# Two-layer hybrid block on one core: another written order in the mixer, and raw compressed keys copied out of their bank

## The chip, the cores and the metric

The kernel runs on one core of one Trainium2 chip. The metric is the device time of one launch in microseconds (us), lower is better. Times of the kernel before come from three timed runs and from one execution recorded by the hardware profiler.

## What is computed

The reference is a two-layer block over 256 tokens of width 1024. Cut to what matters here:

```python
for l in range(2):
    x = x + 0.5 * swiglu_ffn(x, ...)                 # 1024 -> 2816 -> 1024
    h = rms_norm(x, mix_norm[l])
    o_a = fox_mixer(...)      # 4 heads, softmax with a forget bias        (jobs F0, F1)
    o_b = gmlp_mixer(...)     # gated unit with a 128x128 token mix
    o_c = nsa_mixer(...)      # selected + window softmax (jobs N0..N3) and attention to 15 compressed keys
    o_d = pool_mixer(...)     # moving averages, then a product
    x = x + concat(o_a, o_b, o_c, o_d) @ w_out[l]
    x = x + 0.5 * swiglu_ffn(x, ...)

# compressed keys and values, inside nsa_mixer
flat  = blocks_of_32_tokens + pos_emb                # 15 x 2048
k_cmp = rope(rms_norm(gelu(flat_k @ k_w1) @ k_w2))   # 15 x 64
v_cmp = gelu(flat_v @ v_w1) @ v_w2
p_cmp = softmax(q @ k_cmp.T, masked);  o_cmp = p_cmp @ v_cmp
```

With 256 tokens and blocks of 64 every block is among the top ones, so the selection needs no gather: job pairs N0/N1 and N2/N3 are the selected and the window branch of two heads each.

## The kernel before

Each layer is FFN, mixer, FFN. A 32-bit weight tile is loaded by SP's queue, copied into a rounded half `h` on ScalarE (L122), and the rest `lo` is formed on VectorE (L123). TensorE then takes three products per pair of tiles (`mm3`, L143 to L145) or two passes (`mm2x2`, L151 and L153). `raws` holds 4 loaded tiles, `spl` 4 split ones, and `banks` the 8 accumulator banks, which `bank_a` and `bank_h` hand out; a tile waits for a bank until every reader of an earlier tile in it is through.

In the mixer small blocks of attention lie between blocks of long products that need nothing from them. A softmax job goes through six steps: `scores` (eight TensorE instructions into two banks L774, then maxima on VectorE L782 and exponentials with sums on ScalarE L784), `scale` (L790 to L795, VectorE), `trans` (six transpose passes L802 into two banks, copied to memory by ScalarE L804), `values` (L814), `done` (the accumulator is split into halves for the output product, L134 on ScalarE and L135 on VectorE). The compressed branch runs over `cmp_hidden` (four loads and product groups, L462), `cmp_gelu`, `cmp_out` (values into `vbd`, L505; raw keys, their squares L511, and after a `yield` their scaling and rotation L514 to L522), `cmp_keys` (L527), `cmp_scores` (L731 to L751), `cmp_weights` (L758).

The long blocks are generators: `go(w00, 4)` takes the next four steps of `out_part(0, 0)`, twelve products. The first step of `out_part` (and of `b_proj`, `z_proj`) only loads and splits the weights. `w00` and `w10` use the gate and pool outputs (`oT` 2, 3, then 6, 7), `w01` and `w11` use the fox outputs (`oT` 0, 1) and then the compressed/selected/window outputs (`oT` 4, 5). `wacc` and `wacc1` are the two pairs of banks for the output product.

From `here` to `pin(here)` each instruction on TensorE, VectorE and ScalarE is chained behind the one written before it on the same engine, so the written order is the order of these three queues. Instructions written after that stretch (the splits of the next FFN) are not chained and may be put between. SP and GpSimd are not chained.

Of the kernel before, what the change touches and what calls it, by code (L numbers as in the profile page):

```python
# [70 lines left out]
def tile_macaron(ctx, tc, xT, g0, const0, consts, params, w13, w2, wA, wB, wD, wC, wE, wcmp, wo, out):  # L71
# [15 lines left out]
    def bank_a():  # L87
        a = banks.tile([128, 512], F32, name="a", tag="bank")
        return a

    def bank_h():
        h = banks.tile([128, 512], F32, name="h", tag="bank")
        return h
# [5 lines left out]
    def halves(s):  # L99
        return s.rearrange("p (a n) -> p a n", a=2)  # L100
# [87 lines left out]
    def inv_rms(ss, n, width, p=128):  # L188

        ms = wk.tile([128, 16], F32)  # L190
        nc.gpsimd.tensor_scalar(ms[:p, :width], ss, 1.0 / n, EPS, op0=ALU.mult, op1=ALU.add)
        iv = wk.tile([128, 16], F32)
        nc.gpsimd.tensor_tensor(iv[:p, :width], ms[:p, :width], mhalf[:p, :width], op=ALU.pow)
        return iv[:p, :width]
# [157 lines left out]
    def mixer(l, norm, par):  # L352
        def Pm(name, p=128):
            o, w = _PAR[name]
            return par[0:p, o:o + w]
# [141 lines left out]
        def cmp_out():  # L497
            cw2 = Pm("cw2").rearrange("p (a h d) -> p a h d", a=2, h=2)
            pv = bank_h()
            for hb in range(2):  # L500
                nc.tensor.matmul(pv[:, 0:64], e.chv[:, hb].rearrange("p g n -> p (g n)"), cw2[:, 1, hb, :],
                                 start=hb == 0, stop=hb == 1)
            for g in range(4):
                rows = slice(32 * g, 32 * g + 32)
                nc.vector.tensor_copy(vbd[rows, g // 2, 64 * (g % 2):64 * (g % 2) + 64], pv[rows, 0:64])  # L505
            pkc = bank_h()
            for hb in range(2):
                nc.tensor.matmul(pkc[0:NC, 0:64], e.ch[:, hb, 0:NC], cw2[:, 0, hb, :], start=hb == 0, stop=hb == 1)
            kss = wk.tile([128, 1], F32)
            kcn = w1p.tile([16, 128], F32)  # L510
            nc.scalar.activation(kcn[0:NC, 64:128], pkc[0:NC, 0:64], AF.Square, accum_out=kss[0:NC, :])  # L511
            kiv = inv_rms(kss[0:NC, :], 64, 1, NC)
            yield
            nc.vector.scalar_tensor_tensor(kcn[0:NC, 0:64], pkc[0:NC, 0:64], kiv, Pm("kcn", NC), op0=ALU.mult,  # L514
                                           op1=ALU.mult)
            cr = C("crope", NC).rearrange("p (a c) -> p a c", a=2)
            ct = w1p.tile([16, 32], F32)
            nc.vector.tensor_tensor(ct[0:NC, 0:16], kcn[0:NC, 0:16], cr[:, 0, :], op=ALU.mult)
            nc.vector.tensor_tensor(ct[0:NC, 16:24], kcn[0:NC, 8:16], cr[:, 1, 0:8], op=ALU.mult)
            nc.vector.tensor_tensor(ct[0:NC, 24:32], kcn[0:NC, 0:8], cr[:, 1, 8:16], op=ALU.mult)  # L520
            nc.vector.tensor_tensor(kcn[0:NC, 0:16], ct[0:NC, 0:16], ct[0:NC, 16:32], op=ALU.add)
            nc.vector.tensor_copy(kcn[0:NC, 64:128], kcn[0:NC, 0:64])  # L522
            e.kcn = kcn
# [104 lines left out]
        def b_post():  # L628
            nt = head_norm(e.pB, e.hB, 6, 384)
            nqk = w1p.tile([128, 2, 448], F32)  # L630
            nq = nqk[:, :, 0:384].rearrange("p t (h d) -> p t h d", d=64)
            for t in range(2):
                nc.vector.tensor_tensor(nqk[:, t, 0:384], nt[t][:, 0:384], Pm("ngain"), op=ALU.mult)
            ra = w1p.tile([128, 2, 6, 16], F32)
            rc = w1p.tile([128, 2, 6, 16], F32)

            def tab(i, c0, c1):
                return rope[:, i, :, c0:c1].unsqueeze(2).to_broadcast([128, 2, 6, c1 - c0])

            nc.vector.tensor_tensor(ra, nq[:, :, :, 0:16], tab(0, 0, 16), op=ALU.mult)  # L640
            nc.vector.tensor_tensor(rc[:, :, :, 0:8], nq[:, :, :, 8:16], tab(1, 0, 8), op=ALU.mult)
            nc.vector.tensor_tensor(rc[:, :, :, 8:16], nq[:, :, :, 0:8], tab(1, 8, 16), op=ALU.mult)
            nc.vector.tensor_tensor(nq[:, :, :, 0:16], ra, rc, op=ALU.add)
            nc.vector.tensor_copy(nqk[:, :, 384:448], nqk[:, :, 256:320])
            e.nqk = nqk
# [120 lines left out]
        tcols = (slice(0, 128), slice(128, 384))  # L766

        def scores(jb):

            q, ks = jb.qk()  # L770
            s = [bank_h(), bank_h()]
            for t, c in enumerate(tcols):
                for i, rows in enumerate(half_rows):
                    nc.tensor.matmul(s[i][:, c], q[rows, 128 * t:128 * t + 128], ks[i][rows, 0:128 * t + 128],  # L774
                                     start=True, stop=True)
            bias = e.bias[jb.pair] if jb.branch is None else [(mask[:, 128:256], mask)] * 2
            jb.s = [s2(), s2()]
            jb.sm = at.tile([128, 2, 2], F32, name="sm")
            nm = at.tile([128, 2, 2], F32, name="nm")
            for i in range(2):  # L780
                for t, c in enumerate(tcols):
                    nc.vector.tensor_tensor_reduce(out=jb.s[i][:, c], in0=s[i][:, c], in1=bias[i][t], op0=ALU.add,  # L782
                                                   op1=ALU.min, scale=-1.0, scalar=3e38, accum_out=nm[:, t, i:i + 1])
                    nc.scalar.activation(jb.s[i][:, c], jb.s[i][:, c], AF.Exp, scale=-1.0, bias=nm[:, t, i:i + 1],  # L784
                                         accum_out=jb.sm[:, t, i:i + 1])

        def scale(jb):

            rv = at.tile([128, 2, 2], F32, name="rv")
            nc.vector.reciprocal(rv, jb.sm)  # L790
            if jb.branch is not None:
                nc.vector.tensor_tensor(rv, rv, e.g4[:, :, 2 * jb.pair:2 * jb.pair + 2, jb.branch], op=ALU.mult)
            for i in range(2):
                for t, c in enumerate(tcols):
                    nc.vector.tensor_scalar(jb.s[i][:, c], jb.s[i][:, c], rv[:, t, i:i + 1], None, op0=ALU.mult)  # L795
# [36 lines left out]
        def out_part(d, q, accs):  # L832

            h, lo = split(wo[l, d, q], 2048)
            yield
            for c, kk in [(c, kk) for k2 in (0, 2) for c in range(4) for kk in (k2, k2 + 1)]:
                s = slice(512 * kk + 128 * c, 512 * kk + 128 * c + 128)
                mm3(accs[c // 2][:, c % 2, :], (h[:, s], lo[:, s]), oT[_KORD[4 * q + kk]],
                    q == 0 and kk == 0 and c % 2 == 0, q == 1 and kk == 3 and c % 2 == 1)
                yield  # L840
# [16 lines left out]
        def go(gen, n=1):  # L857
            for _ in range(n):
                next(gen, None)
# [12 lines left out]
        go(bq, 3)  # L872
        c_heads()
        wacc = [halves(bank_a()), halves(bank_a())]
        w00, w01 = out_part(0, 0, wacc), out_part(0, 1, wacc)
        go(w00)
        go(bq, 2)
        cmp_hidden(0, 1)
        b_stats()
        scores(F0)  # L880
        go(zq)
        fox_bias(1)
        cmp_hidden(1, 0)
        scale(F0)
        b_post()
        scores(F1)
        go(zq)
        trans(F0)
        b_heads()
        cmp_hidden(1, 1)  # L890
        pool_mix()
        scale(F1)
        values(F0)
        scores(N0)
        gelu = cmp_gelu()
        go(gelu)
        trans(F1)
        go(w00, 4)
        done(F0)
        go(gelu)  # L900
        scale(N0)
        pool_out()
        values(F1)
        scores(N1)
        go(w01)
        done(F1)
        go(w00, 4)
        go(gelu)
        trans(N0)
        scale(N1)  # L910
        go(w00, 4)
        values(N0)
        scores(N2)
        go(w00, 5)
        outs = cmp_out()
        go(outs)
        trans(N1)
        wacc1 = [halves(bank_a()), halves(bank_a())]
        w10, w11 = out_part(1, 0, wacc1), out_part(1, 1, wacc1)
        go(w10)  # L920
        go(w01, 4)
        go(outs)
        values(N1)
        scale(N2)
        scores(N3)
        go(w01, 4)
        trans(N2)
        cmp_keys()
        go(w10, 3)
        cs = cmp_scores()  # L930
        go(cs)
        scale(N3)
        go(w11)
        go(w10, 1)
        values(N2)
        go(cs)
        go(w10, 4)
        trans(N3)
        go(w10, 5)
        go(cs)  # L940
        values(N3)
        go(w10, 4)
        cmp_weights()
        go(w11, 4)
        done(N1)
        done(N3)
        go(w11, 4)
        pin(here)
# [132 lines left out]
```

## Time and profile before

| what | value |
|---|---|
| median of 3 runs | 976.45 us (975.28 to 977.28) |
| the profiled execution's own time | 975.51 us |
| its span in the profile | 973.7 us |
| TensorE busy | 958.2 us, 98% |
| VectorE busy | 697.6 us, 72% |
| ScalarE busy | 531.0 us, 55% |
| HBM read | 177.27 MB, 183 GB/s over the span |

The profiled execution is 0.94 us shorter than the median. A busy TensorE here means that a matmul was in flight, also at the lower of the clock's two levels; the granted clock of a stretch is shown as a share of 2.4 GHz, so 0.50 is 1.2 GHz. Idle time of an engine that others do not wait for costs nothing. The mixer's chained stretch runs from about 229 to 299 us in the first layer and from about 710 to 779 us in the second.

### The profile page before, as it was taken

How to read it: one execution, taken by the hardware profiler on the slowest of the kernel's cores; microseconds unless marked ns; L12 is line 12 of the kernel's file. 1: busy time of each engine (PE TensorE's matmuls, PEld its weight loads, DVE VectorE, ACT ScalarE, POOL GpSimd, SP SyncE). 2: the span in 40 equal slices, each digit the busy share in tenths (PEclk: the TensorE clock that was granted, in tenths of full speed). 3: DMA queues.
4: the chain of work that ended last, by engine and by line, in shares of the span. 5: the costliest groups of instructions: out<-in, count | busy, mean ns of one | idle time of the engine just before them, and what ended most of it. 6: DMA issues, size and time to landing. Idle time of an engine off the chain costs nothing. (4 is left out here: it accounts for less than half of the span.)

```text
span 973.7 us, 14899 instructions
## 1 busy us (share of the span) xinstructions
PE 958.2 (98%) x5840; PEld 834.9 (86%) x5840; DVE 697.6 (72%) x1256; ACT 531.0 (55%) x971; POOL 68.0 (7%) x67
## 2 busy tenths in 40 slices
PE   9999999999989999999999999999998999999998
PEld 6888888898878888888888888889987898888887
DVE  5988776575778788786668787765666787878751
ACT  7666555363556565654545655544545665565540
POOL 2000000041102000000010000001220030000000
PEclk9999999999989999999999999999999999999999
DMA  8965554545426655555555555544553455555530
GB/s 308 342 243 183 179 208 155 169 140 214 174 87 221 240 188 179 207 177 187 203 173 178 207 177 186 203 153 158 197 208 111 152 208 183 179 203 181 178 108 17
DMA packets 28150, 179.28 MB, mean 184 GB/s; under 512 B 3248, under 2 KB 5168, under 8 KB 8240
## 3 DMA queue, kind: packets, MB, share of 16 engines
q1 hardware_dynamic: 27792, 178.19, 52.4%
q8 instruction: 46, 0.75, 0.3%
q10 hardware_dynamic: 288, 0.14, 0.1%
q14 instruction: 24, 0.20, 0.0%
HBM read 177.27 MB, written 1.05 MB: 183 GB/s over the span
## 5 line engine op out<-in xcount | busy, mean ns | idle before, releaser
L123 DVE TENSOR_TENSOR lo<-r,h 128x1024 fp32r<-128x1024 f32 (+4 forms) x346 | 395.4, 1158 | 156.0 <-ACT h L122 155.8
L122 ACT ACTIVATE h<-r 128x1024 fp32r<-128x1024 f32 (+4 forms) x346 | 328.3, 974 | 261.6 <-issue 225.5
L151 PE MATMUL h<-hl,h 128*128 128x512 f32 x1408 | 443.5, 396 | 0.8 <-DVE hl L138 0.5
L153 PEld LDWEIGHTS h<-hl,lo 128*128 128x128 f32 x1408 | 264.2, 188 | 64.2 <-DVE lo L123 2.0
L153 PE MATMUL h<-hl,lo 128*128 128x256 f32 x1408 | 277.1, 278 | 0.3 <-DVE lo L123 0.3
L151 PE MATMUL a<-hl,h 128*128 128x512 f32 x704 | 221.9, 396 | 0.0
L151 PEld LDWEIGHTS h<-hl,h 128*128 128x128 f32 x1408 | 214.6, 189 | 1.9 <-DVE hl L138 1.2
L153 PEld LDWEIGHTS a<-hl,lo 128*128 128x128 f32 x704 | 132.1, 188 | 30.9
L153 PE MATMUL a<-hl,lo 128*128 128x256 f32 x704 | 138.7, 278 | 0.0
L151 PEld LDWEIGHTS a<-hl,h 128*128 128x128 f32 x704 | 107.5, 189 | 1.3 <-DVE hl L135 1.2
L238 DVE SCALAR_TENSOR_TENSOR x<-a,x 128x256 f32<-128x256 f32 x80 | 32.9, 421 | 51.2 <-PE a L153 47.5
L306 DVE TENSOR_TENSOR s<-h,s 128x256 f32<-128x256 f32 x176 | 65.8, 415 | 0.0
L307 DVE TENSOR_TENSOR s<-s,rb 128x512 f32<-128x512 f32 x88 | 60.8, 691 | 2.8
L134 ACT ACTIVATE hl<-s 128x256 fp32r<-128x256 f32 x92 | 38.2, 417 | 43.6 <-DVE s L310 34.1
L215 POOL TENSOR_TENSOR s<-s 128x512 f32<-128x512 f32 x12 | 17.1, 1429 | 587.2 <-ACT s L211 587.2
L305 ACT ACTIVATE s<-h 128x256 f32<-128x256 f32 x176 | 56.5, 372 | 0.0
L143 PE MATMUL a<-h,hl 128*128 128x384 f32 (+2 forms) x128 | 45.8, 357 | 0.0
L145 PE MATMUL a<-h,hl 128*128 128x384 f32 (+2 forms) x128 | 45.0, 351 | 0.0
L309 ACT ACTIVATE s<-s 128x256 f32<-128x256 f32 x88 | 35.5, 403 | 17.3 <-DVE s L307 17.3
L144 PE MATMUL a<-lo,hl 128*128 128x384 f32 (+2 forms) x128 | 44.9, 351 | 0.0
L135 DVE TENSOR_TENSOR hl<-s,hl 128x256 fp32r<-128x256 f32 x92 | 38.3, 419 | 3.4 <-ACT hl L134 3.4
L143 PE MATMUL a<-hl,h 128*128 128x256 f32 x128 | 39.3, 307 | 0.1
(187 smaller groups left out, 776.7 us busy)
## 6 DMA issues: line engine op xcount, KB each, us to landing
r<-in_w_dram SPq DMA_DIRECT2D x129, 1024.0 KB, 4.8
r<-in_wcmp_dram SPq DMA_DIRECT2D x8, 1024.0 KB, 4.9
r<-in_wo_dram SPq DMA_DIRECT2D x8, 1024.0 KB, 5.0
r<-in_wE_dram SPq DMA_DIRECT2D x4, 1024.0 KB, 4.8
r<-in_wC_dram SPq DMA_DIRECT2D x4, 1024.0 KB, 4.8
r<-in_wD_dram SPq DMA_DIRECT2D x4, 800.0 KB, 4.4
r<-in_wA_dram SPq DMA_DIRECT2D x4, 768.0 KB, 4.4
r<-in_wB_dram SPq DMA_DIRECT2D x4, 768.0 KB, 4.3
```

Source lines behind the costliest of these rows:

```text
L122: nc.scalar.activation(h[:, c], r[:, c], AF.Copy)
L123: nc.vector.tensor_tensor(lo[:, c], r[:, c], h[:, c].bitcast(F32), op=ALU.subtract)
L134: nc.scalar.activation(th, src, AF.Copy)
L135: nc.vector.tensor_tensor(tl, src, th.bitcast(F32), op=ALU.subtract)
L143: nc.tensor.matmul(o, wgt[0], mov[0], start=start, stop=False)
L144: nc.tensor.matmul(o, wgt[0], mov[1], start=False, stop=False)
L145: return nc.tensor.matmul(o, wgt[1], mov[0], start=False, stop=stop)
L151: nc.tensor.matmul(o, wgt[0], mov[2], start=start, stop=False)
L153: ins = nc.tensor.matmul(o[:, :T], wgt[1], mov[0], start=False, stop=stop)
L305: nc.scalar.activation(hr[:, j, :], st[m][j][:, T:], AF.Copy)
L306: nc.vector.tensor_tensor(hr[:, j, :], st[m][j][:, :T], hr[:, j, :], op=ALU.add)
L307: nc.vector.tensor_tensor(hr, hr, st["rb"].unsqueeze(1).to_broadcast([128, 2, T]), op=ALU.mult)
```

## The change

`scores` is cut in two: the products stay in `scores`, and the maxima and exponentials become `softmax`. The order of the stretch is written anew. `scale`, `trans` and `values` of a job, the splits of `w01`, `w10` and `w11`, the steps of the compressed branch and the allocation of `wacc1` stand at other places; every step is still there once. In `cmp_out` ScalarE copies the raw keys from their bank to `kcn`, and the scaling reads them there.

```diff
             nc.scalar.activation(kcn[0:NC, 64:128], pkc[0:NC, 0:64], AF.Square, accum_out=kss[0:NC, :])
+            nc.scalar.activation(kcn[0:NC, 0:64], pkc[0:NC, 0:64], AF.Copy)
             kiv = inv_rms(kss[0:NC, :], 64, 1, NC)
             yield
-            nc.vector.scalar_tensor_tensor(kcn[0:NC, 0:64], pkc[0:NC, 0:64], kiv, Pm("kcn", NC), op0=ALU.mult,
+            nc.vector.scalar_tensor_tensor(kcn[0:NC, 0:64], kcn[0:NC, 0:64], kiv, Pm("kcn", NC), op0=ALU.mult,
                                            op1=ALU.mult)
...
         def scores(jb):
-
             q, ks = jb.qk()
-            s = [bank_h(), bank_h()]
+            jb.p = s = [bank_h(), bank_h()]
...
+        def softmax(jb):
+
+            s = jb.p
             bias = e.bias[jb.pair] if jb.branch is None else [(mask[:, 128:256], mask)] * 2
...
         wacc = [halves(bank_a()), halves(bank_a())]
+        wacc1 = []
         w00, w01 = out_part(0, 0, wacc), out_part(0, 1, wacc)
+        w10, w11 = out_part(1, 0, wacc1), out_part(1, 1, wacc1)
         go(w00)
         go(bq, 2)
         cmp_hidden(0, 1)
         b_stats()
         scores(F0)
+        softmax(F0)
         go(zq)
         fox_bias(1)
         cmp_hidden(1, 0)
         scale(F0)
+        scores(F1)
+        trans(F0)
+        softmax(F1)
         b_post()
-        scores(F1)
         go(zq)
-        trans(F0)
-        b_heads()
+        values(F0)
         cmp_hidden(1, 1)
         pool_mix()
         scale(F1)
-        values(F0)
-        scores(N0)
+        b_heads()
         gelu = cmp_gelu()
         go(gelu)
         trans(F1)
+        done(F0)
+        scores(N0)
+        softmax(N0)
+        go(gelu)
         go(w00, 4)
-        done(F0)
-        go(gelu)
+        values(F1)
         scale(N0)
         pool_out()
-        values(F1)
+        go(w01)
+        go(w00, 4)
         scores(N1)
-        go(w01)
+        go(w00, 4)
+        trans(N0)
+        softmax(N1)
+        go(gelu)
         done(F1)
-        go(w00, 4)
-        go(gelu)
-        trans(N0)
         scale(N1)
-        go(w00, 4)
+        go(w10)
+        go(w00, 5)
         values(N0)
         scores(N2)
-        go(w00, 5)
+        go(w01, 2)
         outs = cmp_out()
         go(outs)
+        go(w01, 2)
         trans(N1)
-        wacc1 = [halves(bank_a()), halves(bank_a())]
-        w10, w11 = out_part(1, 0, wacc1), out_part(1, 1, wacc1)
-        go(w10)
+        softmax(N2)
+        go(outs)
+        scale(N2)
         go(w01, 4)
-        go(outs)
         values(N1)
-        scale(N2)
+        wacc1 += [halves(bank_a()), halves(bank_a())]
+        go(w10, 2)
+        cmp_keys()
         scores(N3)
-        go(w01, 4)
+        go(w10, 2)
         trans(N2)
-        cmp_keys()
+        softmax(N3)
+        cs = cmp_scores()
+        go(cs, 2)
+        scale(N3)
+        go(cs)
+        go(w11)
+        go(w10, 4)
+        values(N2)
         go(w10, 3)
-        cs = cmp_scores()
-        go(cs)
-        scale(N3)
-        go(w11)
-        go(w10, 1)
-        values(N2)
-        go(cs)
+        trans(N3)
+        go(w10, 2)
+        cmp_weights()
         go(w10, 4)
-        trans(N3)
-        go(w10, 5)
-        go(cs)
+        done(N1)
         values(N3)
-        go(w10, 4)
-        cmp_weights()
         go(w11, 4)
-        done(N1)
         done(N3)
         go(w11, 4)
         pin(here)
```

## Rows read from the trace of the kernel before

**Rows 1.** Waits of TensorE over the whole span: us in total, times, longest us.

```profile
PE a L814 <- ACT s L804: 6.0, 4, 2.6
PE h L802 <- DVE s L795: 2.1, 2, 1.0
PE h L606 <- ACT s L596: 0.7, 2, 0.3
```

**Rows 2.** Busy time by stretch, first layer; columns PE, PEld, DVE, ACT, POOL, then PEclk.

```profile
271.00:277.00 6.00, 6.00 (x32) 4.73 (x30) 4.11 (x21) 1.86 (x8) 0.00 (x0) 0.53 0.51 175
280.00:286.00 6.00, 4.92 (x40) 3.75 (x37) 5.78 (x24) 1.92 (x6) 0.00 (x0) 1.00 0.46 147
```

**Rows 3.** The same view, second layer.

```profile
751.00:754.00 3.00, 2.77 (x14) 2.08 (x16) 2.86 (x11) 0.55 (x2) 0.00 (x0) 0.51 0.32 71
```

**Rows 4.** TensorE in order of time, first layer: start, us, line, operands, count [idle <-releaser].

```profile
270.51 1.92 PE L814 MATMUL a<-s 128*64 128x256 f32 x8 [2.64 <-ACT s L804]
...
273.94 0.58 PE L143 MATMUL a<-hl,h 128*128 128x256 f32 x1
...
276.65 0.56 PE L501 MATMUL h<-par,chv 128*128 128x64 f32 x4
...
279.70 0.87 PE L814 MATMUL a<-s 128*64 128x256 f32 x8
...
281.36 0.38 PE L143 MATMUL a<-hl,h 128*128 128x256 f32 x1
...
282.76 0.28 PE L145 MATMUL a<-hl,lo 128*128 128x256 f32 x1
284.08 1.07 PE L802 MATMUL h<-c0t,s 128*128 128x128 f32 x6 [1.04 <-DVE s L795]
...
293.12 1.25 PE L814 MATMUL a<-s 128*64 128x256 f32 x8 [0.36 <-ACT s L804]
```

**Rows 5.** The same view, second layer.

```profile
751.23 1.92 PE L814 MATMUL a<-s 128*64 128x256 f32 x8 [2.64 <-ACT s L804]
...
754.60 0.39 PE L143 MATMUL a<-hl,h 128*128 128x256 f32 x1
```

**Rows 6.** ScalarE in order of time, first layer.

```profile
267.84 1.99 ACT L122 ACTIVATE h<-r 128x1024 fp32r<-128x1024 f32 x2
269.73 0.36 ACT L134 ACTIVATE hl<-a 128x256 fp32r<-128x256 f32 x1
270.00 0.84 ACT L804 ACTIVATE s<-h 128x384 f32<-128x384 f32 x2
...
277.57 0.21 ACT L511 ACTIVATE kcn<-h 15x64 f32<-15x64 f32 x1 [1.32 <-PE h L508]
```

**Rows 7.** VectorE in order of time, first layer.

```profile
248.80 1.01 DVE L795 TENSOR_SCALAR s<-s,rv 128x128 f32<-128x128 f32 x4
...
268.91 2.36 DVE L123 TENSOR_TENSOR lo<-r,h 128x1024 fp32r<-128x1024 f32 x2 [1.98 <-ACT h L122]
...
271.52 0.18 DVE L486 TENSOR_SCALAR g<-g 128x60 f32<-128x60 f32 x1
...
272.67 0.17 DVE L790 RECIPROCAL rv<-sm 128x4 f32<-128x4 f32 x1
...
274.05 0.29 DVE L782 CUSTOM_DVE_ANT_0 s<-h,cst 128x128 f32<-128x128 f32 x1
...
277.24 0.92 DVE L505 COPY vbd<-h 32x64 f32<-32x64 f32 x4 [2.00 <-PE h L501]
...
282.29 0.27 DVE L514 SCALAR_TENSOR_TENSOR kcn<-h,iv,par 15x64 f32<-15x64 f32 x1
...
283.26 0.16 DVE L790 RECIPROCAL rv<-sm 128x4 f32<-128x4 f32 x1
```

**Rows 8.** VectorE: an FFN split among steps of `cmp_scores`, and the first residual sum.

```profile
291.48 0.68 DVE L123 TENSOR_TENSOR lo<-r,h 128x512 fp32r<-128x512 f32 x1
...
301.05 0.76 DVE L238 SCALAR_TENSOR_TENSOR x<-a,x 128x256 f32<-128x256 f32 x2 [1.43 <-PE a L145]
```

## Prediction

> **What bounds the kernel now.** TensorE is busy for 98% of the span, so the page alone promises little. I read its list of waits first: nearly all idle time of a bound engine should stand there. It has four waits for transposed weights (L804, 6.0 us), two for scaled scores (L802, 2.1) and two for the pool input (L606, 0.7), 8.8 us in all, half of it in each layer's mixer [rows 1]. Then the busy time by stretch with its clock, because a busy engine at 1.2 GHz hides loss: behind the longest wait the granted clock is 0.53 of 2.4 GHz in the first layer and 0.51 in the second [rows 2, 3]. Behind the 1.04 us wait it is 1.00 [rows 2]. Last, the order of time on TensorE prices the slow stretch. `values` with `scores` take 281.36 − 279.70 = 1.66 us at full clock, and 273.94 − 270.51 = 3.43 behind the wait; the twelve products after them take 276.65 − 273.94 = 2.71, against 282.76 + 0.12 − 281.36 = 1.52. So the clock costs 1.77 + 1.19 = 3.0 us in the first layer [rows 4]. In the second it is back by 754.60: 754.60 − 751.23 = 3.37, less 1.66, is 1.7 [rows 5].
>
> Why the long wait? `values(N0)` needs the copies of `trans(N0)`, and on ScalarE these stand behind `w01`'s split (1.99 us) and `done(F1)` (0.36): they begin at 270.00 [rows 6]. TensorE is through with its cover at about 267.9 and idles 2.64 us [rows 4]. It is the written order that makes this wait, not a lack of work.
>
> **What the change removes.** In the new order `w01`'s split is queued before `trans(N0)` and its work runs while TensorE has two blocks of four steps and `scores(N1)` (1.52 + 1.52 + 0.8), and four steps more lie between `trans(N0)` and `values(N0)`. By the durations below, the copies end about 0.9 us before `values(N0)` is reached. The 2.64 goes, and with it the slow clock. `trans(N2)` waits now for a scaling that stands behind `w10`'s split and the raw keys, at 284.08 [rows 4]; its scores will be scaled one block earlier. `values(N3)` (0.36) gets five more steps and `cmp_weights` as cover, `pool_mix` (0.33) gets `values(F0)` and `cmp_hidden(1, 1)`, some 1.8. Two of these blocks also run long from a second, shorter wait inside: 1.25 against 0.87 for `values(N3)`, 0.38; for `trans(N2)` 1.07, where an undisturbed one takes about 0.7 (an estimate), 0.35 [rows 4]. Per layer: 2.64 + 1.04 + 0.36 + 0.33 + 0.73 = 5.1, in two layers 10.2; with the clock 3.0 + 1.7 it is 14.9 us, the most that this change can win.
>
> **What it puts in their place, per layer.**
> (a) `trans(F0)` comes right behind `scores(F1)`, at about 249.2, while VectorE scales F0's scores from 248.80 to 249.81 [rows 7]. The first half can start at 249.3. For the second half the banks run out: `b_proj` holds two, `wacc` two, `cmp_hidden` one, F1's scores two, the first half one, that is eight. `b_post` and `softmax(F1)`, which free some, stand behind the scaling on VectorE. The second half waits until about 250.3 for the first maxima or the first copy. Bounds 0.3 (a bank free at once) and 1.3 (the later release); I take 0.9, near the copy of 0.84/2 that must pass [rows 6].
> (b) The second step of `w01` needs `done(F1)`, now behind the gelu steps: 0 to 0.3, I take 0.1.
> (c) `cmp_keys` needs the rotated raw keys. From the end of `trans(F1)` to it TensorE has three pairs of `values` and `scores` (3 × 1.66 = 5.0), 26 steps (6.5 × 1.52 = 9.9) and four small blocks (`pool_out`, `cmp_out`, two `trans`; an estimate of 0.75 each, 3.0): 17.9. In this time the other two engines must do, one behind the other: F1's copies and `done(F0)`, 0.84 + 0.36 + 0.35 = 1.5; three times the maxima (about 1.2 each, four reductions of which the first takes 0.29), 3.6; one wait for exponentials, 1.0; two scalings, 2 × (274.05 − 272.67) = 2.8; `pool_out`'s two splits, which take turns at one bank, 1.3; `w01`'s first half copy, 1.0; two weight splits, 2 × 2.3 = 4.6; the gelu's last step, 272.67 − 271.52 = 1.15; `done(F1)` 0.65; `vbd` 0.92; the keys, 283.26 − 282.29 = 0.97. Sum 19.5 [rows 6, 7]. That leaves a wait of 1.6; laying the same pieces out along the clock, with the overlaps that the queues allow, I get 0.7 to 1.1. I take 1.0, bounds 0 and 2.6.
> (d) At `trans(N2)` eight banks are taken again (`wacc` two, `wacc1` two, one accumulator, the key transpose, N3's scores two), and the transposes wait for the first of N3's maxima: 0 to 0.7, I take 0.3.
> (e) At the end `trans(N3)`'s copies stand behind `w11`'s split and perhaps the next FFN's pieces, on VectorE 0.68 each [rows 8]: 0 to 1.1, I take 0.2.
> Together 2.5 per layer, 5.0 in both, bounds 0.6 and 12.
>
> **What costs nothing.** The added copy of the raw keys is like the 0.21 us of L511 [rows 6], between that and `trans(N1)`'s copies, with four steps and 1.5 us of TensorE before `values(N1)`; without that cover it would cost its 0.2. Its bank comes free at once, otherwise `trans(N1)` would wait for the keys' scaling. `b_post` behind `softmax(F1)` has until `b_heads`, three blocks on. Loads: SP's queue has the same loads in the same order; a split made earlier frees its loaded tile earlier, so the next loads start earlier. GpSimd gets no new work. Behind the mixer VectorE waits 1.43 us for TensorE before the first residual sum [rows 8], and it gets the FFN's splits done sooner too, so I let the gain through in full.
>
> **Sum.** 975.51 − 14.9 + 5.0 = 965.6 us for the profiled execution. The median of the three runs is 0.94 higher, in a spread of 2.0, which may be another slow stretch of the sort that goes. I forecast 966.0.
>
> **The rivals.**
> A, TensorE's wait moves to the keys. VectorE is nearly full from `w01`'s split to `scale(N3)`. If (c) is not 1.0 but the 2.64 that dropped the clock in both layers [rows 2 to 5], each layer pays 1.64 and 1.7 to 3.0 more: 966 + 6.7 to 9.3, about 974. For it: the sum in (c) says 1.6. Against: the overlaps.
> B, short waits drop the clock. In the trace a wait of 1.04 left the clock at 1.00 [rows 2], but the new order makes four short waits, two of them at banks. Were one to cost what the second layer paid, 1.7, or the first, 3.0 [rows 4, 5], it would be 969.4 to 972. The Trainium skill, "TensorE: Matmul & The Clock Gate", "A second HAM failure mode: psum-queue depth-cycling", describes such a case: short idles at cycled banks made the clock swing with no long gap. By that rule this rival holds; the row at 1.00 speaks against it.
> C, slower: splits of the next FFN get ahead of the keys. They are not chained, and before they slip in between dependent steps of VectorE, 0.68 each [rows 8]. `w00` ends much earlier now and gives its split buffer free earlier. Four pieces before `cmp_keys` lengthen its wait by 2.7 and bring the slow clock, 3.0: the new cost is 8.2 per layer where 7.45 was removed, about 977.5; eight pieces, 983. It decides from four pieces on. Against: before, they came only behind `w11`'s split, and that stays late.
> D, no difference: the waits are as long in sum as before, at other places, or the queues don't take the written order: 975 to 977. Against: the chain to `pin`.
> E, none of the new waits shows: 966 − 5.0 = 961.
>
> **Chances.** Forecast 0.56, A 0.15, B 0.07, C 0.09, D 0.07, E 0.06. The range from 961.5 to 974.5 leaves out D, C and the ends of A and E, 2 in 10. About 0.2%, 2 us, is what a measurement of this kernel can tell from no change: faster is the forecast, B, E and nearly all of A, 0.83; same 0.08; slower 0.09.
>
> **What would show it.** Right: no wait at `values(N0)`, clock 1.00 through both mixers, about 2.5 us of waits per layer at `trans(F0)` and `cmp_keys`, and the mixer's stretch shorter by some 6 us in the first layer and 4 to 5 in the second. Wrong: a wait above 2 us at `cmp_keys` (A, C), a clock of 0.5 behind short waits (B), or a wait at the FFN's first products, where I let the gain through.

## The result and the profile after

| | before | after |
|---|---|---|
| median (lowest to highest), us | 976.87 (975.28 to 977.73), 4 runs | 962.93 (962.56 to 963.09), 4 runs |
| profiled execution, us | 975.51, its span 973.7 | 963.09, its span 961.3 |

The ratio is 0.9865, interval 0.9852 to 0.9877: 13.9 us by the medians, 12.4 by the two profiled executions. The forecast was 966.0, in a range of 961.5 to 974.5.

First the list of TensorE's waits in the kernel after (line waited at, who releases it: us in total, times, longest). Of the three mixer lines of [rows 1] none is left; these two are new, and they are all that the mixer has:

```profile
PE h L528 <- DVE kcn L523: 1.0, 2, 0.5
PE h L732 <- ACT s L808: 0.5, 2, 0.3
```

L528 is the transpose in `cmp_keys`, L732 the products of `cmp_scores`. Then the same stretch of each layer by landmarks, from the first product of `fox_bias(1)` to the first product of the FFN, in TensorE's order of time (start, busy us, engine, line, operation). Before:

```profile
246.80 0.60 PE L699 MATMUL h<-c0t,ncc 128*128 128x128 f32 x4
...
305.17 0.63 PE L151 MATMUL h<-hl,h 128*128 128x512 f32 x2
...
727.51 0.60 PE L699 MATMUL h<-c0t,ncc 128*128 128x128 f32 x4
...
784.65 0.63 PE L151 MATMUL h<-hl,h 128*128 128x512 f32 x2
```

After:

```profile
246.98 0.60 PE L700 MATMUL h<-c0t,ncc 128*128 128x128 f32 x4
...
298.44 0.63 PE L151 MATMUL h<-hl,h 128*128 128x512 f32 x2
...
720.77 0.60 PE L700 MATMUL h<-c0t,ncc 128*128 128x128 f32 x4
...
772.22 0.63 PE L151 MATMUL h<-hl,h 128*128 128x512 f32 x2
```

The first layer took 305.17 − 246.80 = 58.37 and takes 51.46; the second took 57.14 and takes 51.45. That is 6.91 and 5.69 us, 12.6 together, and the spans differ by 12.4: the whole gain is in the two mixers, and the two layers, which differed by 1.2 before, are now alike. The clock says why. Windows of the kernel after over both mixers (from:to, length, busy time of PE, PEld, DVE, ACT and POOL with instructions, granted clock, DMA share, GB/s):

```profile
240.00:293.00 53.00, 52.26 (x462) 43.88 (x461) 42.36 (x149) 36.30 (x99) 5.24 (x6) 1.00 0.47 168
714.00:767.00 53.00, 52.26 (x463) 43.93 (x462) 42.36 (x149) 36.29 (x99) 4.92 (x5) 1.00 0.48 167
```

It is 1.00 over both mixers, where [rows 2] and [rows 3] had 0.53 and 0.51 behind the long wait. Taking off the 3.0 and 1.7 us that the slow clock cost by [rows 4, 5], the waits gave 6.91 − 3.0 = 3.9 and 5.69 − 1.7 = 4.0 per layer. The prediction took away 5.1 of them, so new ones cost some 1.2 per layer, not 2.5.

Who does the work that TensorE no longer waits for? The windows over 262 to 286 us, before and then after:

```profile
262.00:286.00 24.00, 20.28 (x143) 16.19 (x142) 17.14 (x70) 11.94 (x36) 1.04 (x3) 0.86 0.25 82
```

```profile
262.00:286.00 24.00, 23.26 (x195) 19.84 (x190) 20.32 (x83) 16.55 (x49) 2.51 (x3) 1.00 0.25 89
```

The columns for VectorE and ScalarE (third and fourth busy times) rise from 17.14 to 20.32 and from 11.94 to 16.55 us of 24. Before, VectorE had 6.9 us free in a stretch in which TensorE waited at the end of chains that run over VectorE. The single pieces, in the kernel after (idle time before a group and its releaser in brackets):

```profile
249.37 1.12 PE L806 MATMUL h<-c0t,s 128*128 128x128 f32 x6
250.24 0.37 PE L143 MATMUL h<-h,hl 128*128 128x256 f32 x1
...
267.25 0.82 PE L806 MATMUL h<-c0t,s 128*128 128x128 f32 x6
267.83 0.36 PE L143 MATMUL a<-hl,h 128*128 128x256 f32 x1
...
269.43 0.87 PE L818 MATMUL a<-s 128*64 128x256 f32 x8
...
277.95 0.20 PE L528 MATMUL h<-c0t,kcn 15*128 15x15 f32 x1 [0.49 <-DVE kcn L523]
279.76 0.82 PE L806 MATMUL h<-c0t,s 128*128 128x128 f32 x6
280.83 1.08 PE L732 MATMUL h<-kcz,s 128*128 128x30 f32 x8 [0.25 <-ACT s L808]
...
267.78 0.87 ACT L808 ACTIVATE s<-h 128x384 f32<-128x384 f32 x2 [0.84 <-PE h L806]
...
266.02 2.36 DVE L123 TENSOR_TENSOR lo<-r,h 128x1024 fp32r<-128x1024 f32 x2 [0.46 <-ACT h L122]
...
277.62 0.18 DVE L523 COPY kcn<-kcn 15x64 f32<-15x64 f32 x1
...
249.36 0.88 PEld L806 LDWEIGHTS h<-c0t,s 128*128 128x128 f32 x6 [0.33 <-DVE s L799]
```

`values(N0)` (269.43) starts with no idle time ahead of it, since `trans(N0)`'s copies (ACT L808) start at 267.78, not at the 270.00 of [rows 6]. `w01`'s split is on VectorE at 266.02, where [rows 7] had it at 268.91.

### The profile page after: what moved, and what is told of

It reads as the page before. It is cut to its first block, busy times and chain, and to the rows that moved or that the text cites. A ratio compares the mean times of both kernels' runs of the same rounds, so it can differ in the third digit from the quotient of the medians.

```text
span 961.3 us, 14890 instructions
## 1 busy us (share of the span) xinstructions
PE 952.3 (99%) x5840; PEld 831.8 (87%) x5840; DVE 698.8 (73%) x1256; ACT 532.7 (55%) x973; POOL 70.9 (7%) x67
## 4 chain that ended last, share of the span: by engine, by line
PE 95%; DVE 2%; ACT 1%; DMA 1%; issue 0%; SPq 0%; POOL 0%
PE h L151 33%; PE a L151 17%; PE h L153 17%; PE a L153 8%; PE a L143 4%; PE a L145 4%; PE a L144 4%; DMA x<-in_xT_dram 1%; PE h L774 1%; PE h L143 1%; PE h L462 1%; PE h L144 1%; PE h L145 1%; PE a L818 1%; PE h L806 1%; DVE lo L123 1%
## 5 line engine op out<-in xcount | busy, mean ns | idle before, releaser
L134 ACT ACTIVATE hl<-s 128x256 fp32r<-128x256 f32 x92 | 38.2, 417 | 43.6 <-DVE s L310 34.1
```

The source lines that it names most:

```text
L134: nc.scalar.activation(th, src, AF.Copy)
```

## The experiments

In the diffs a minus is the kernel named, a plus the experiment. All kernels compute the whole output. "Before" is the median of its runs beside them. Three theories: the reading in the prediction, that the long wait comes from ScalarE's order, in which `trans(N0)`'s copies stand behind `w01`'s split, and that removing it pays (T1); that it is VectorE, which idles in one place and is late in the next, so that the place of the pieces on VectorE counts (T2); that the gain is the copy of the raw keys (T3).

**Only `trans(N0)` moved**, in the kernel before.

```diff
-        go(w01)
-        done(F1)
-        go(w00, 4)
-        go(gelu)
         trans(N0)
+        go(w01)
+        done(F1)
+        go(w00, 4)
+        go(gelu)
         scale(N1)
```

> The kernel before with one edit: trans(N0) is written ahead of go(w01) and done(F1), nothing else. Theory (the long wait is made by the copies standing behind w01's split on ScalarE, and the slow clock by the wait): the wait at values(N0) shrinks from 2.64 us to about 0.8, the granted clock stays at 1.00 through both mixers, and each layer gains 1.85 us of wait plus the clock's 3.0 or 1.7: 8 us in all, about 968.5. Rival 1 (the wait only moves, since w01's split is needed soon after): under 3 us of gain. Rival 2 (the clock falls for another reason, a mixer's mean load): the waits shrink, the clock falls all the same, 3.7 us of gain, about 973.

978.09 us (976.04 to 981.12) against 975.59: ratio 1.0024, interval 1.0009 to 1.0038. TensorE's and VectorE's order of time in the first layer, and the windows with the clock (third figure from the right):

```profile
267.53 1.24 PE L814 MATMUL a<-s 128*64 128x256 f32 x8 [0.51 <-ACT s L804]
...
272.69 0.63 PE L501 MATMUL h<-par,chv 128*128 128x64 f32 x4 [1.46 <-DVE chv L493]
...
282.20 1.06 PE L802 MATMUL h<-c0t,s 128*128 128x128 f32 x6 [1.25 <-DVE s L795]
...
268.83 2.36 DVE L123 TENSOR_TENSOR lo<-r,h 128x1024 fp32r<-128x1024 f32 x2 [2.73 <-ACT h L122]
...
273.00:276.00 3.00, 2.81 (x17) 2.24 (x17) 2.90 (x16) 1.75 (x8) 0.41 (x1) 0.61 0.71 300
285.00:288.00 3.00, 3.00 (x15) 2.72 (x16) 0.97 (x5) 3.00 (x6) 0.00 (x0) 0.50 0.03 5
```

T1 is right about the wait itself: at `values(N0)` it shrinks from 2.64 to 0.51. It fails as the reason for the gain: it gave 968.5, and the kernel is slower, if anything. `w01`'s split starts at 268.83, as late as in [rows 7]; VectorE stands idle 2.73 us ahead of it and gets to everything behind it no earlier. TensorE meets the same lateness in smaller pieces, 1.46 at `cmp_out` and 1.25 at `trans(N2)`. And the clock falls twice, to 0.61 and 0.50, with no wait above 1.46 us in this mixer.

**The new order without the copy.**

```diff
-            nc.scalar.activation(kcn[0:NC, 0:64], pkc[0:NC, 0:64], AF.Copy)
...
-            nc.vector.scalar_tensor_tensor(kcn[0:NC, 0:64], kcn[0:NC, 0:64], kiv, Pm("kcn", NC), op0=ALU.mult,
+            nc.vector.scalar_tensor_tensor(kcn[0:NC, 0:64], pkc[0:NC, 0:64], kiv, Pm("kcn", NC), op0=ALU.mult,
```

> The changed kernel with the copy of the raw keys undone: the scaling reads them from their bank again, in the new order. Theory (the copy frees a bank that trans(N1) needs): the second half of trans(N1) waits for a bank; if it is the raw keys' own, until about 277.0 in the first layer, 3 us, and the clock may fall, so 6 to 12 us slower than the changed kernel, 969 to 975. Rival (another bank comes free first, that of the first half of trans(N1) at about 274.4 or that of the compressed values at 275.7): 0.5 to 1.8 us at trans(N1), most of it given back at cmp_keys, where TensorE waits for VectorE anyway: within 1.5 us of the changed kernel.

963.31 us (962.57 to 965.0), ratio 0.9873, interval 0.9858 to 0.9888, against 0.9865 with the copy. TensorE's order of time:

```profile
274.13 0.55 PE L805 MATMUL h<-c0t,s 128*128 128x128 f32 x3 [0.58 <-ACT s L807]
...
277.76 0.23 PE L527 MATMUL h<-c0t,kcn 15*128 15x15 f32 x1
```

The second half of `trans(N1)` waits 0.58 us for the copy that frees the bank of its first half, so one bank is missing; `cmp_keys` then has no wait where it had 0.49. The two nearly cancel. T3 is out: without the copy the kernel is 0.4 us slower by the medians, a difference that the runs don't resolve.

**The copy alone**, in the kernel before.

```diff
+            nc.scalar.activation(kcn[0:NC, 0:64], pkc[0:NC, 0:64], AF.Copy)
...
-            nc.vector.scalar_tensor_tensor(kcn[0:NC, 0:64], pkc[0:NC, 0:64], kiv, Pm("kcn", NC), op0=ALU.mult,
+            nc.vector.scalar_tensor_tensor(kcn[0:NC, 0:64], kcn[0:NC, 0:64], kiv, Pm("kcn", NC), op0=ALU.mult,
```

> The kernel before with only the copy of the raw keys added, in the old order. Theory: the copy of some 0.2 us lies beside other work and its bank is not asked for, so no change, 976.9 within 1 us, which is the spread of that kernel's runs. Rival (the copy pays by itself): over 2 us faster. The other rival: 0.2 us slower per layer.

974.36 us (973.03 to 977.48), ratio 0.9987, interval 0.9973 to 1.0001: no difference that can be told. Its waits and the window behind the first layer's long one:

```profile
PE a L815 <- ACT s L805: 6.0, 4, 2.6
...
269.00:272.00 3.00, 1.70 (x14) 1.24 (x16) 2.96 (x5) 1.62 (x4) 0.00 (x0) 1.00 0.00 0
```

The four waits at `values` are those of [rows 1], to the tenth, yet in this execution the clock is 1.00 around the first layer's and falls only in the second. The long wait does not always bring the slow clock.

**The new order's first half**: as after up to `scores(N1)`, `trans(N0)` and `done(F1)`, as before from `scale(N1)` on; the copy stays.

```diff
         go(w01)
-        done(F1)
         go(w00, 4)
-        go(gelu)
+        scores(N1)
         trans(N0)
+        softmax(N1)
+        go(gelu)
+        done(F1)
         scale(N1)
         go(w00, 4)
```

> The new order up to scores(N1), then the old order from scale(N1) to the end (trans(N0) right behind scores(N1), ahead of four steps of w00; the copy of the raw keys stays). Theory: the first half of the order holds the long wait, its clock and the pool input's wait; the second half the waits at trans(N2) and values(N3). So this kernel wins 2.64 + 0.33 less 0.3 (trans(F0)) per layer and the clock, with a wait of at most 0.8 left at values(N0): 8.5 to 10 us, about 967.5, and keeps the waits of about 1.0 at trans(N2) and 0.4 at values(N3). Rival (the second half of the order is what pays): under 4 us of gain.

969.79 us (969.45 to 971.81), ratio 0.9944, interval 0.9926 to 0.9961: 5.8 us of the 13.3 that both halves give (975.83 − 962.57, further down), and less than the 8.5 to 10 expected. TensorE's order of time:

```profile
279.93 1.16 PE L806 MATMUL h<-c0t,s 128*128 128x128 f32 x6 [1.55 <-DVE s L799]
```

The waits of 2.64 are gone, and the clock is 1.00 in three of its four runs; but with the later steps in the old order VectorE comes to N2's scores late, and 1.55 us of wait stand at `trans(N2)`, where [rows 4] had 1.04. The lateness moved on, as with `trans(N0)` alone. `w01`'s split is early here too (VectorE takes it up at 265.19), so its place alone does not make the whole gain.

**The second half**: the old order up to `values(N0)`, with `w10`'s split behind `scale(N1)`, and the new one from `cmp_out` on.

```diff
         trans(N0)
         scale(N1)
+        go(w10)
         go(w00, 4)
         values(N0)
...
         go(w00, 5)
+        go(w01, 2)
         outs = cmp_out()
```

> The old order up to values(N0) (only go(w10) stands behind scale(N1)), the new order from cmp_out to the end; the copy of the raw keys is in. Theory (the waits at trans(N2) and values(N3) are the second half's own): the 2.64 us at values(N0) and the falls of the clock stay, the waits of 1.04 + 0.35 and 0.36 + 0.38 go, and the one at cmp_keys is covered by the time lost before: some 4 us of gain, 971 to 973, with a mean granted clock below 1.00 in the runs. Rival (the halves only pay together, since VectorE's chain runs through both): under 1.5 us of gain.

970.43 us (968.86 to 971.02) against 975.83, ratio 0.9939, interval 0.9921 to 0.9958: 5.4 us, where some 4 was expected. Order of time, and a window behind the second layer's wait:

```profile
269.82 1.24 PE L818 MATMUL a<-s 128*64 128x256 f32 x8 [2.64 <-ACT s L808]
...
746.00:750.00 4.00, 3.81 (x18) 2.44 (x19) 3.86 (x14) 2.40 (x4) 0.00 (x0) 0.57 0.52 162
```

The 2.64 at `values(N0)` is there in both layers, the waits at `trans(N2)` and `values(N3)` are not. The clock falls in the second layer only. The halves give 5.8 + 5.4 = 11.2 us apart and 13.3 together.

**`w01`'s split back behind `trans(N0)`**, one line of the kernel after.

```diff
         pool_out()
-        go(w01)
         go(w00, 4)
         scores(N1)
         go(w00, 4)
         trans(N0)
+        go(w01)
         softmax(N1)
```

> The changed kernel with one line moved: go(w01), the load and split of w01, behind trans(N0) instead of ahead of the eight steps of w00. Theory (what pays in the new order is that w01's split fills VectorE's idle time; behind trans(N0) VectorE idles until about 269.7 in the first layer, and all that follows on it comes 3.7 us later): waits of about 3.4 us per layer at the second step of w01 and at cmp_out, and the clock falls: 973 to 981, as slow as the kernel before. Rival (the place of the copies of trans(N0) on ScalarE, ahead of w01's split here as there, is what pays): within 2 us of the changed kernel.

972.34 us (971.66 to 974.4) against 975.62, ratio 0.9966, interval 0.9954 to 0.9979. The order of time on TensorE, ScalarE and VectorE, and windows with the clock:

```profile
274.94 0.39 PE L143 MATMUL a<-hl,h 128*128 128x256 f32 x1 [2.72 <-ACT hl L134]
...
272.76 0.40 ACT L788 ACTIVATE s<-s,nm 128x128 f32<-128x128 f32 x1 [1.69 <-DVE nm L786]
...
270.15 2.36 DVE L123 TENSOR_TENSOR lo<-r,h 128x1024 fp32r<-128x1024 f32 x2 [4.07 <-ACT h L122]
...
262.00:286.00 24.00, 20.95 (x156) 17.34 (x154) 17.25 (x71) 13.15 (x40) 2.47 (x3) 0.93 0.26 88
276.00:279.00 3.00, 3.00 (x17) 2.74 (x17) 3.00 (x5) 1.20 (x4) 1.98 (x3) 0.55 0.20 82
754.00:757.00 3.00, 3.00 (x18) 2.68 (x17) 3.00 (x6) 1.35 (x4) 1.42 (x1) 0.52 0.24 101
```

This line gives back 972.34 − 962.93 = 9.4 of the 13.9 us. VectorE idles 4.07 us ahead of the split, its busy time in the window is back at 17.25 (17.14 before), and the split starts at 270.15 instead of 266.02. N1's maxima stand behind it on VectorE, ScalarE waits 1.69 us for them before N1's exponentials (272.76), and `done(F1)` (ACT L134) stands behind those: TensorE waits 2.72 us for it at `w01`'s second step, in both layers, and the clock falls to 0.55 and 0.52 after it. So some 5 of the 9.4 are the two waits, and the rest is for the most part the clock (an estimate). `trans(N0)`'s copies are ahead of the split here, and `values(N0)` has no wait; still most of the gain is gone. T2 holds: within this order it counts that the split falls into VectorE's idle time ahead of `trans(N0)`. The run moves ScalarE's part of the split along with VectorE's; that VectorE's part is the one that holds things up is read from the 1.69 us, and no run moves the split alone in the kernel before.

**More work on VectorE ahead of the keys**: two needless additions of 128x512, in the kernel after.

```diff
         softmax(N2)
+        extra = s2()
+        for _ in range(2):
+            nc.vector.tensor_tensor(extra, C("band")[:, 0:512], C("band")[:, 512:1024], op=ALU.add)
         go(outs)
```

> The changed kernel with two needless additions of 128x512 on VectorE (some 0.65 us each, 1.3 in all per layer) between N2's maxima and the scaling of the raw keys. Theory (VectorE sets the time at cmp_keys, one for one): 1.3 us of wait more there in each layer, 2.6 us slower, about 965.5, and the clock stays at 1.00 if waits of that size alone don't drop it; 969 to 972 if it falls. Rival (VectorE has slack): under 0.8 us.

966.5 us (965.96 to 969.49), ratio 0.9915, interval 0.9889 to 0.994; 3.6 us above the kernel after. TensorE's order of time and a window in each layer:

```profile
278.48 0.20 PE L528 MATMUL h<-c0t,kcn 15*128 15x15 f32 x1 [1.82 <-DVE rv L794]
...
280.00:282.00 2.00, 2.00 (x12) 1.95 (x10) 1.15 (x8) 0.25 (x1) 0.00 (x0) 0.50 0.00 0
756.00:760.00 4.00, 3.75 (x31) 3.51 (x32) 2.50 (x15) 2.79 (x11) 0.00 (x0) 1.00 0.01 4
```

The wait at `cmp_keys` grows from 0.49 to 1.82 in each layer, 1.33 more: VectorE has no slack left ahead of the keys. In this execution the clock falls to 0.50 behind the first layer's 1.82 and stays at 1.00 behind the second's, and the landmarks price it: the second layer takes 775.36 − 722.57 = 52.79, 1.34 more than in the kernel after, which is the wait; the first takes 300.22 − 246.18 = 54.04, 2.58 more, so the clock cost 1.2.

**Cover for the keys**, in the kernel after: `cmp_keys` and `scores(N3)` behind four steps of `w10`.

```diff
-        go(w10, 2)
+        go(w10, 4)
         cmp_keys()
         scores(N3)
-        go(w10, 2)
         trans(N2)
```

> The changed kernel with cmp_keys and scores(N3) behind four steps of w10 instead of two. Theory (VectorE's chain to the rotated keys is the bound at this place, by 0.5 us of idle and some 0.65 in all): the wait at cmp_keys vanishes, and unless it comes back at trans(N2), whose scaling is done 1.3 us after the keys, the kernel gains 0.5 to 1.3 us over both layers: 961.7 to 962.5. Rival (the wait moves to trans(N2) in full): 962.9.

961.78 us (961.22 to 962.33), ratio 0.9859, interval 0.9835 to 0.9884. The list of waits has no line of the mixer any more. By the medians the gain is 962.93 − 961.78 = 1.15 us, but the two kernels were not run beside each other and the intervals of their ratios overlap, so the times alone don't show it. The landmarks do, here in the first layer:

```profile
247.36 0.60 PE L700 MATMUL h<-c0t,ncc 128*128 128x128 f32 x4
...
298.23 0.63 PE L151 MATMUL h<-hl,h 128*128 128x512 f32 x2
```

That is 50.87 where the kernel after has 51.46, 0.59 less, and as much in the second layer. The waits of 0.49 and 0.25 would give 0.74; the next experiment shows where some of it went.

**Cover for all three places**, in the kernel after; run twice, the second time beside the kernel after itself.

```diff
-        trans(F0)
         softmax(F1)
         b_post()
         go(zq)
-        values(F0)
+        trans(F0)
         cmp_hidden(1, 1)
+        values(F0)
...
-        go(w10, 2)
+        go(w10, 4)
         cmp_keys()
         scores(N3)
-        go(w10, 2)
         trans(N2)
         softmax(N3)
+        go(w10, 2)
         cs = cmp_scores()
...
         go(w11)
-        go(w10, 4)
+        go(w10, 2)
```

> The changed kernel with each of its three remaining short waits given cover: trans(F0) again behind z_proj's second half, cmp_keys behind four steps of w10, and cmp_scores behind two steps more. Theory (the new order's waits are 0.3 at trans(F0), 0.65 at cmp_keys and 0.35 at cmp_scores per layer, and nothing else is late behind them): 2.0 to 2.6 us faster than the changed kernel, about 960.6. Rival (VectorE is the bound from w01's split to N3's scaling, so that the wait reappears at trans(N2) or trans(N3)): 962 to 963.

961.16 us (960.78 to 961.69), ratio 0.9853, interval 0.9829 to 0.9878: 1.8 us below the 962.93, where 2.0 to 2.6 was expected.

> The changed kernel as it is, beside the next run on one chip: 962.9 within 0.6 us, its clock at 0.999 to 1.00 in each run.

> The changed kernel with cover at trans(F0), cmp_keys and cmp_scores, beside the changed kernel on one chip. Theory (the three waits are 1.2 us per layer and gone): 1.2 to 2.4 us faster than the changed kernel. Rival (the 1.8 us between them so far is the difference of two chips): within 0.6 us.

Beside each other: the kernel after 962.57 us (962.44 to 963.54), ratio 0.9863 (0.9846 to 0.9881), and the covered one 960.95 (960.37 to 961.2), ratio 0.9843 (0.9826 to 0.986). The two sets of runs don't overlap: 1.6 us, and the quickest of the kernels here. That is inside the 1.2 to 2.4 expected, but the three waits add up to 1.2 per layer. By the landmarks the covered mixer takes 297.41 − 246.88 = 50.53, 0.93 less than the kernel after. Some of it has come back inside `trans(N2)`, in the covered kernel's order of time on TensorE, products and weight loads (PEld):

```profile
278.67 1.12 PE L806 MATMUL h<-c0t,s 128*128 128x128 f32 x6
279.79 0.39 PE L143 MATMUL a<-hl,h 128*128 128x256 f32 x1
...
278.66 0.31 PEld L806 LDWEIGHTS h<-c0t,s 128*128 128x128 f32 x3 [0.33 <-DVE s L799]
279.24 0.31 PEld L806 LDWEIGHTS h<-c0t,s 128*128 128x128 f32 x3 [0.26 <-PE h L806]
```

From its start to the next step are 1.12 us, where `trans(N0)` of the kernel after takes 0.58: its second half comes late, behind 0.26 of idle time of the weight loads. The list of waits misses this, since TensorE's products were still in flight. What the second half waits for is not shown; the prediction's (d) had a missing bank there. So this wait, too, moved in part. TensorE's busy time in 276 to 284 us, after and then covered:

```profile
276.00:284.00 8.00, 7.26 (x63) 5.94 (x59) 6.34 (x36) 5.57 (x20) 0.00 (x0) 1.00 0.31 126
```

```profile
276.00:284.00 8.00, 7.94 (x64) 6.52 (x63) 6.29 (x36) 5.56 (x20) 0.00 (x0) 1.00 0.30 120
```

It goes from 7.26 to 7.94 of 8 us, with VectorE and ScalarE as busy as they were.

## Why the prediction was right, and where it was not

**The sum.** The places of the waits and the price of the clock carried it. All five removed waits are gone and the clock is 1.00, so the 14.9 us were won as reckoned; the cost was 1.2 per layer instead of 2.5, and the gain 12.4 in the profiled executions instead of 9.9. The clock's 4.7 of it is a price of that one execution: with the same long waits the copy alone and the second half lost the clock in one layer only. By medians it is 13.9 instead of 10.5, because the profiled execution of before lies below its median.

**(a) `trans(F0)`, 0.9, mis-sized.** From its start at 249.37 to the next step at 250.24 are 0.87 us, where `trans(N0)`, with no wait, takes 267.83 − 267.25 = 0.58: 0.3, the lower bound. It runs beside VectorE's scaling of these scores (L799, from 248.98 to 249.99), which also ends the 0.33 of idle time ahead of its weight loads (PEld, 249.36); that the scaling makes the 0.3 is read from these times. A wait for a bank does not show. My count had `wacc`'s two as taken from their allocation, and in the trace they are first written at 259.95; that this frees them is argued and not shown.

**(b) `w01`'s second step, 0.1, and (e) the end, 0.2.** No wait at either.

**(c) `cmp_keys`, 1.0.** The right place and the right cause: 0.49 of idle time, some 0.65 from start to start with the neighbouring steps. The two additions lengthen it one for one, so VectorE's sum ahead of the keys is the bound, as reckoned; the 1.0 that I took was 0.35 too high, well inside its bounds, and the sum's own 1.6 was 0.95 too high.

**(d) `trans(N2)`, 0.3, at another place.** The transposes have no wait, 279.76; the 0.25 stand one step on, at `cmp_scores`, behind the copies of that `trans` on ScalarE.

**The reason for the long wait held, but it is not the reason for the gain.** I wrote that the place of `trans(N0)`'s copies behind `w01`'s split on ScalarE makes the wait. Moving `trans(N0)` alone takes 2.1 us of it away and leaves the time at a ratio of 1.0024. The prediction's sum held all the same, because it priced the whole order; a reader who took its reason for a recipe would have moved one block and gained nothing. With the rest of the new order in place, the place of `w01`'s split is worth 9.4 us. Such prices don't add up: the first half of the order, with the split early, gives 5.8, and the second, with the split late, 5.4.

**"With it the slow clock" was too simple.** The clock fell with waits of 0.51, 1.46 and 1.25, and stayed up in one layer each of two executions behind a wait of 2.64. I take it that the step survives because the order took away nearly all the waits, not one long one.

**The copy.** I wrote that without it `trans(N1)` would wait for the keys' scaling. In the run without it, the second half of `trans(N1)` waits for the copies of its own first half, 0.58, given back at `cmp_keys`. "Costs nothing" fits the runs, the sentence on the bank does not.

**The gain went through in full**, as I let it: VectorE waits for TensorE before the first residual sum after as it did before, 0.53 where [rows 8] had 1.43, and TensorE's FFN starts earlier by the whole amount (landmarks above). The last splits of the mixer (128x1024) and the first of the FFN (128x512), in VectorE's order of time after:

```profile
285.42 3.56 DVE L123 TENSOR_TENSOR lo<-r,h 128x1024 fp32r<-128x1024 f32 x4
...
289.77 2.49 DVE L123 TENSOR_TENSOR lo<-r,h 128x512 fp32r<-128x512 f32 x4
...
294.32 0.76 DVE L238 SCALAR_TENSOR_TENSOR x<-a,x 128x256 f32<-128x256 f32 x2 [0.53 <-PE a L145]
```

**The rivals.** A came as 0.49, not 2.64; the experiment with two additions shows a smaller case of it, 3.6 us by the medians for 1.33 more of wait per layer. B did not happen here, 1.00 throughout, but it is a real mechanism of this kernel: the moved `trans(N0)` met it, with no wait above 1.46 in its first mixer. The Trainium skill, "TensorE: Matmul & The Clock Gate", "A second HAM failure mode: psum-queue depth-cycling", tells of short idles, with banks that are cycled, that make the clock swing. The 0.61 and 0.50 behind waits of 1.46 and 1.25 us agree with it as to short idles, but these waits were for results of VectorE (L493, L795), not for banks; the changed kernel, with waits of 0.5 and less, stays at 1.00. C did not come: the FFN's splits begin at 289.77, behind the mixer's own and 12 us behind the keys. D is out by the ratio. E, 961, did not come either. That the three covers end at 960.95 is luck and no proof of E's sum: E took off 5.0 for the new waits, and the covers gave 1.6.

## What to carry to other kernels

When the bound engine waits at the end of a chain, look for the idle stretch of the engine that feeds the chain, and put a large piece that depends on nothing recent, such as a weight split, into it: here that was worth 9.4 us with the rest of the order in place, while moving the waiting block alone only moved the wait. Price the clock as its own term, and count on it only where hardly any wait is left. Afterwards put the bound engine's independent steps in front of each wait that stayed; here three such moves gave 1.6 us of the 2.4 that the waits came to.

## What the runs showed of the hardware

The kernel before varies with the clock it is granted. In 40 of its timed runs (the 17, 14 and 9 beside the experiments) the times go from 973.10 to 978.36 us and the mean granted clock from 0.992 to 0.998; means of the runs at one clock are 977.73 at 0.992, 974.68 at 0.996 and 973.73 at 0.998. A straight line through them falls by 0.7 us for each 0.001 and would be at 972.0 at 1.000 (an estimate, beyond the last run, and a rough one: the means at 0.994 and 0.995, 975.37 and 976.25, lie off it by up to 0.9). By it some 9 of the gain are waits and 4 to 5 the clock. The kernel after has 0.999 to 1.00 in each run and 962.44 to 963.54 us: the change took away most of the spread as well.

What decides whether the clock falls stays open. It fell behind a wait of 2.64 us in both layers of one execution and in one layer of two others, behind 2.72 in both layers (`w01`'s split late), behind 1.82 in one of two layers, and with the moved `trans(N0)`, with waits of 0.5 to 1.8, in both; behind 1.55 at `trans(N2)`, in the first half's profiled execution, it stayed at 1.00 in both. Open as well are the copy's worth, which the runs don't resolve, why the second half of `trans(F0)` met no wait for a bank, and what that of `trans(N2)` waits for in the covered kernel.
